# A second MLP's up projection in seven block products instead of eight, in three of its four quarters

## The chip, the core and the metric

The kernel runs on one core of a Trainium2 chip. The metric is the device time of one execution in microseconds (us). The core's engines are named as in the profile: PE (matrix products), with its weight loads shown apart as PEld; DVE, ACT and POOL (elementwise work); SP (it issues DMAs). Each engine takes its instructions strictly in the order of its own program and waits on semaphores.

## The reference, cut to what matters

The reference is a decoder of two layers on 512 positions (SEQ) of width 1024 (D_MODEL); each layer ends in a squared-ReLU MLP of width 4096 (D_FF):

```python
def squared_relu_mlp(h, w_up, w_down):
    return jnp.square(jax.nn.relu(h @ w_up)) @ w_down
...
        x = x + squared_relu_mlp(rmsnorm(x, mlp_norm[layer]), w_up[layer], w_down[layer])
    return x
```

All numbers are float32. The change is in `h @ w_up` of the last layer, a product of 512x1024 by 1024x4096.

## The kernel before, in words

Everything is kept transposed: `self.x` is eight tiles of 128 channels by 512 positions. A float32 product is made from three products of "float32r" halves: each operand is split into a high half (ACT rounds it) and a low half (the rest, a subtraction), and `mm3` issues high x high, high x low and low x high (lines 263, 264, 265). The normalisation's factor per position is applied after the down projection (`r2`, line 1142), so `xg` holds only x times the gain, split in halves.

`mlp(l, ...)` works in four quarters of the hidden width. In a quarter, the up projection makes eight column tiles (`j`): a weight tile of 128x1024 is loaded by SP into a staging buffer (tag `st`, three buffers), `wsplit` makes its halves in a `w` buffer (tag `w`, four buffers; ACT writes the high half, line 256, and DVE or POOL the low half, line 258), 24 matmuls of 128x512 fill one PSUM bank, and ACT and DVE evacuate it (ReLU, square, split into halves; lines 1124, 1125, 300, 301) into `a[j]` (tag `qk`). Then the down projection makes eight tiles (`m`) from the eight `a[j]` in the same way, scales them (1142) and adds them to x (1143). In the second MLP (`l` = 1) the low halves of weights go to DVE and POOL in turn (`"vg"[j % 2]`).

A scheduler of the build places instructions on each engine from this code, and a buffer of a tag goes to the next tile that asks for one when its last reader is done. The only order that counts on the chip is that of each engine's program and of SP's and POOL's DMA issues.

Of the kernel before, what the change touches and what calls it, by code (L numbers as in the profile page):

```python
# [9 lines left out]
F32R = mybir.dt.float32r  # L10
AF = mybir.ActivationFunctionType
ALU = mybir.AluOpType
AX = mybir.AxisListType

P = 128
D = 1024
S = 512
# [16 lines left out]
def bcast(ap, dim, n):  # L34

    a = [list(x) for x in ap.ap]
    a.insert(dim, [0, n])
    return bass.AP(tensor=ap.tensor, offset=ap.offset, ap=a)
# [47 lines left out]
class Work:  # L86
# [5 lines left out]
    def add(self, gen, name=None, when=None):  # L92

        self.q.append(self.mark(self.after(when, gen) if when else gen, name))
# [71 lines left out]
class K:  # L166
    def __init__(self, ctx, tc, ins, out):
# [14 lines left out]
        act=12, st=3, w=4, qk=8, pt4=4, p2=6, raw=2, tmp=3, sq=1, rb=1, tq=2, qki=2, ki=2, x=8, r1=2, r2=2, r3=2, r4=2, r5=2, r6=3, r7=2, nm=8, su=6, cr=6, c1=3, c2=3, nb=4,  # L182
# [3 lines left out]
    def t(self, tag, shape, dt=F32):  # L186
        self.n += 1
        return self.sb.tile(shape, dt, name=f"{self.lab}_{tag}_{self.n}", tag=tag, bufs=self.BUFS[tag])
# [919 lines left out]
    def mlp(self, l, dst, done=None):  # L1108
        nc, ins = self.nc, self.ins
        xg = self.xg(self.x, f"mlp{l}")  # L1110
        side = iter(()) if l else self.presplit()
        r2 = None
        for q in range(4):
            a = []
            for j in range(8):
                w = self.wload(ins["w_up"][l, q * 8 + j], "v" if l == 0 else "vg"[j % 2])
                ps = self.ps(self.pS, [P, S])
                for k in range(KT):
                    self.mm3(
                        ps, [w[:, h, k * P : (k + 1) * P] for h in (0, 1)], [xg[k][:, h, :] for h in (0, 1)],  # L1120
                        k == 0, k == KT - 1,
                    )
                u = self.t("p2", [P, S])
                nc.scalar.activation(u, ps, AF.Relu)  # L1124
                nc.vector.scalar_tensor_tensor(out=u, in0=ps, scalar=0.0, in1=u, op0=ALU.max, op1=ALU.mult)  # L1125
                t = self.t(self.A_TAGS[j], [P, 2, S], F32R)
                self.split(t, u, "v")
                a.append(t)
                if r2 is None:
                    r2 = self.stats_bcast()  # L1130
                elif j % 2:
                    next(side, None)
            for m in range(KT):
                w = self.wload(ins["w_dn"][l, q * 8 + m], "v" if l == 0 else "vg"[m % 2])
                ps = self.ps(self.pS, [P, S])
                for j in range(8):
                    self.mm3(
                        ps, [w[:, h, j * P : (j + 1) * P] for h in (0, 1)], [a[j][:, h, :] for h in (0, 1)],
                        j == 0, j == 7,
                    )  # L1140
                y = self.t("p2", [P, S])
                nc.vector.tensor_tensor(out=y, in0=ps, in1=r2, op=ALU.mult)  # L1142
                nc.vector.tensor_tensor(out=self.x[m], in0=self.x[m], in1=y, op=ALU.add)
                if q < 3 and m < 7:
                    next(side, None)
                if q == 3:
                    nc.sync.dma_start(dst[m], self.x[m])
                    if done:
                        done(m)


    def layer_b(self, xd):
# [415 lines left out]
```

## Time and profile before

| what | us |
|---|---|
| median of three runs | 1364.41 (1364.21 to 1367.28) |
| the profiled execution | 1366.07 |
| its span, first to last instruction | 1364.3 |
| second MLP, from its first matmul to the last (read from the timeline) | about 1008 to 1360 |

The span is what the views below divide; the profiled execution takes 1.8 us more than its span, and is 1.7 us above the median of the runs.

### The profile page before, as it was taken

How to read it: one execution, taken by the hardware profiler on the slowest of the kernel's cores; microseconds unless marked ns; L12 is line 12 of the kernel's file. 1: busy time of each engine (PE TensorE's matmuls, PEld its weight loads, DVE VectorE, ACT ScalarE, POOL GpSimd, SP SyncE). 2: the span in 40 equal slices, each digit the busy share in tenths (PEclk: the TensorE clock that was granted, in tenths of full speed). 3: DMA queues.
4: the chain of work that ended last, by engine and by line, in shares of the span. 5: the costliest groups of instructions: out<-in, count | busy, mean ns of one | idle time of the engine just before them, and what ended most of it. 6: DMA issues, size and time to landing. Idle time of an engine off the chain costs nothing.

```text
span 1364.3 us, 18302 instructions
## 1 busy us (share of the span) xinstructions
PE 1302.6 (95%) x6585; PEld 1071.3 (79%) x6585; DVE 817.3 (60%) x1444; ACT 592.5 (43%) x1364; POOL 461.4 (34%) x574
## 2 busy tenths in 40 slices
PE   7867999999999999999999999999899999999998
PEld 6756887677688888888888788887577888888887
DVE  5976777764588676654555255565578455364452
ACT  6755558674444343321233247666552122222220
POOL 3452684442243333200013576351334222222220
PEclk9987999999999999999999999999999999999999
DMA  6233111012339999923334642224033223223231
GB/s 231 77 101 126 63 40 40 9 34 68 125 115 369 396 316 367 322 98 102 104 117 152 245 151 97 83 90 163 32 123 108 93 93 108 94 94 107 93 107 48
DMA packets 55722, 180.66 MB, mean 132 GB/s; under 512 B 6512, under 2 KB 12656, under 8 KB 54352
## 3 DMA queue, kind: packets, MB, share of 16 engines
q1 hardware_dynamic: 44336, 132.18, 28.4%
q0 software_dynamic: 10720, 46.26, 9.1%
q8 instruction: 52, 0.85, 0.2%
q10 hardware_dynamic: 576, 1.05, 0.2%
q14 instruction: 38, 0.31, 0.1%
HBM read 144.86 MB, written 34.60 MB: 132 GB/s over the span
## 4 chain that ended last, share of the span: by engine, by line
PE 82%; DVE 6%; DMA 5%; ACT 5%; issue 2%; POOL 1%; SPq 0%; ACTq 0%; POOLq 0%; DVEq 0%
PE s_ps L263 19%; PE s_ps L264 19%; PE s_ps L265 19%; PE s_acc L263 4%; PE s_acc L264 4%; PE s_acc L265 4%; PE s_po L1064 2%; DVE s_w L258 1%; DMA s_w<-w_bq 1%; PE s_pt L1051 1%; PE s_ps L1297 1%; PE s_ps L1015 1%; ACT s_w L256 1%; DMA s_st<-in_w_ag_dram 1%; PE s_po L660 1%
## 5 line engine op out<-in xcount | busy, mean ns | idle before, releaser
L256 ACT ACTIVATE s_w<-s_st 128x1024 fp32r<-128x1024 f32 (+2 forms) x182 | 180.4, 996 | 258.2 <-PE s_ps L265 206.3
L263 PE MATMUL s_ps<-s_act,s_w 128*128 128x512 f32 x576 | 223.6, 391 | 1.7 <-ACT s_act L298 1.4
L264 PE MATMUL s_ps<-s_act,s_w 128*128 128x512 f32 x576 | 224.4, 390 | 0.0
L265 PE MATMUL s_ps<-s_act,s_w 128*128 128x512 f32 x576 | 224.1, 390 | 0.0
L258 POOL TENSOR_TENSOR s_w<-s_st,s_w 128x1024 fp32r<-128x1024 f32 (+2 forms) x47 | 105.3, 2242 | 317.7 <-ACT s_w L256 317.7
L264 PE MATMUL s_ps<-s_qk,s_w 128*128 128x512 f32 x512 | 198.5, 389 | 0.0
L265 PE MATMUL s_ps<-s_qk,s_w 128*128 128x512 f32 x512 | 198.5, 389 | 0.0
L263 PE MATMUL s_ps<-s_qk,s_w 128*128 128x512 f32 x512 | 198.1, 389 | 0.0
L258 DVE TENSOR_TENSOR s_w<-s_st,s_w 128x1024 fp32r<-128x1024 f32 (+1 forms) x135 | 164.2, 1221 | 17.7 <-ACT s_w L256 17.1
L1142 DVE TENSOR_TENSOR s_p<-s_ps,s_raw 128x512 f32<-128x512 f32 x64 | 44.2, 691 | 158.3 <-PE s_ps L265 158.3
L1124 ACT ACTIVATE s_p<-s_ps 128x512 f32<-128x512 f32 x64 | 38.2, 598 | 219.8 <-PE s_ps L265 211.8
L263 PEld LDWEIGHTS s_ps<-s_act,s_w 128*128 128x128 f32 x576 | 107.9, 188 | 27.7 <-ACT s_act L298 3.1
L264 PEld LDWEIGHTS s_ps<-s_act,s_w 128*128 128x128 f32 x576 | 108.1, 188 | 23.5 <-issue 0.8
L265 PEld LDWEIGHTS s_ps<-s_act,s_w 128*128 128x128 f32 x576 | 108.1, 188 | 23.2 <-issue 0.8
L263 PE MATMUL s_acc<-s_w,s_act 128*128 128x512 f32 (+3 forms) x304 | 109.6, 363 | 15.7 <-ACT s_w L256 8.3
L1125 DVE SCALAR_TENSOR_TENSOR s_p<-s_ps,s_p 128x512 f32<-128x512 f32 x64 | 44.1, 689 | 122.1 <-ACT s_p L1124 122.1
L263 PEld LDWEIGHTS s_ps<-s_qk,s_w 128*128 128x128 f32 x512 | 96.1, 188 | 20.2
L265 PEld LDWEIGHTS s_ps<-s_qk,s_w 128*128 128x128 f32 x512 | 96.1, 188 | 19.9
L264 PEld LDWEIGHTS s_ps<-s_qk,s_w 128*128 128x128 f32 x512 | 96.1, 188 | 19.9
L264 PE MATMUL s_acc<-s_w,s_act 128*128 128x512 f32 (+3 forms) x304 | 108.4, 357 | 0.7 <-DVE s_w L258 0.6
L265 PE MATMUL s_acc<-s_w,s_act 128*128 128x512 f32 (+3 forms) x304 | 106.4, 354 | 0.0
L696 POOL TENSOR_SCALAR s_p<-s_p,s_cr 128x256 f32<-128x256 f32 (+3 forms) x128 | 69.2, 555 | 79.5 <-DVE s_cr L1027 38.1
(299 smaller groups left out, 2440.2 us busy)
## 6 DMA issues: line engine op xcount, KB each, us to landing
s_st<-in_w_up_dram SPq DMA_DIRECT2D x64, 512.0 KB, 3.5
s_st<-in_w_dn_dram SPq DMA_DIRECT2D x64, 512.0 KB, 3.5
w_bq<-s_pt POOLq DMA_DIRECT2D x32, 384.0 KB, 5.8
s_w<-w_bq SPq DMA_DIRECT2D x16, 768.0 KB, 6.8
w_kv<-s_pt POOLq DMA_DIRECT2D x16, 512.0 KB, 8.5
s_w<-w_kv SPq DMA_DIRECT2D x8, 1024.0 KB, 5.3
s_act<-in_w_bq_dram POOLq DMA_DIRECT2D x16, 384.0 KB, 7.1
w_bo<-s_pt POOLq DMA_DIRECT2D x16, 384.0 KB, 5.8
```

The source lines that it names most:

```text
L256: nc.scalar.activation(w[:, 0], st, AF.Copy)
L258: e.tensor_tensor(out=w[:, 1], in0=st, in1=w[:, 0], op=ALU.subtract)
L263: mm(ps, lh[0], rh[0], start=start, stop=False)
L264: mm(ps, lh[0], rh[1], start=False, stop=False)
L265: mm(ps, lh[1], rh[0], start=False, stop=stop)
L660: nc.tensor.matmul(O[hp * 64 : hp * 64 + 64, :], kf[0][:, kb, 1, hh * HD : (hh + 1) * HD], pT[hh][:, kb, :], start=kb == 0, stop=kb == 1,)
L696: self.nc.gpsimd.tensor_scalar(out=p, in0=p, scalar1=c, scalar2=1.0, op0=ALU.mult, op1=ALU.mult)
L1015: nc.tensor.matmul(Sp, q[:, blk], kk[hl][:, br, 0:n], start=hl == 0, stop=False)
L1064: nc.tensor.matmul(O[x * 64 : x * 64 + 64, q0 + o : q0 + 256], v[:, j, br, :], st[x][br][:, j, o:256], start=half == 0 and br == 0 and j = ...
L1124: nc.scalar.activation(u, ps, AF.Relu)
L1125: nc.vector.scalar_tensor_tensor(out=u, in0=ps, scalar=0.0, in1=u, op0=ALU.max, op1=ALU.mult)
L1142: nc.vector.tensor_tensor(out=y, in0=ps, in1=r2, op=ALU.mult)
```

## The change

In the first quarter nothing changes but that DVE makes all low halves (`"v"`), and that during its down projection `tparts` makes, for four pairs of channel tiles, the four sums of blocks of x*gain that the scheme needs, split in halves; the last of them is written over the second half of `xg[0..3]`. In the other three quarters, `up_pair` makes two column tiles at a time. The product of the pair is seen as 2x2 blocks (channels in two halves, the pair's two columns, positions in two halves of 256), and seven block products of 12 matmuls of 128x256 replace eight: 84 such matmuls in place of 48 of 128x512. For it:

- r is the first column's weights, c a sum of weight blocks that a DMA adds (SP loads the second column into c, then POOL issues a DMA that accumulates two blocks onto it), d a half of the second column, loaded once more into a `qki` buffer;
- `w1`, `w3` and `w4` are the split halves of r, of c, and of r after two additions on DVE (line 1204 of the new file); `w2` those of d;
- the products are added up from PSUM on DVE (line 1204), and ACT makes ReLU and square (1236 to 1243) ahead of the usual split.

PE takes the products in this order: p1 (w1), two with w3 into `p75`, two into `p26` (w1, w4), two into `p43` (w2, w4).

```diff
-                w = self.wload(ins["w_up"][l, q * 8 + j], "v" if l == 0 else "vg"[j % 2])
+            if T:
+                for j in range(0, 8, 2):
+                    a += self.up_pair(l, q * 8 + j, xg, T, self.A_TAGS[j : j + 2])
+            for j in range(0 if not T else 8, 8):
+                w = self.wload(ins["w_up"][l, q * 8 + j], "v")
...
             for m in range(KT):
-                w = self.wload(ins["w_dn"][l, q * 8 + m], "v" if l == 0 else "vg"[m % 2])
+                if l and q == 0 and m < 4:
+                    T.append(self.tparts(xg, m, self.gcol(f"mlp{l}")))
+                w = self.wload(ins["w_dn"][l, q * 8 + m], "v")
...
+    def tparts(self, xg, k, g):
...
+        b1, b2 = [self.t("p2", [P, S]) for _ in range(2)]
+        nc.scalar.activation(b1, self.x[k], AF.Copy, scale=g[:, k : k + 1])
+        nc.scalar.activation(b2, self.x[k + 4], AF.Copy, scale=g[:, k + 4 : k + 5])
...
+    def up_pair(self, l, m, xg, T, tags):
...
+        r = self.wdma(src)
+        c = self.t("st", [P, 2, H * 2])
+        two = lambda a, step: bass.AP(tensor=a.tensor, offset=a.offset, ap=[list(a.ap[0]), [step, 2], [1, 512]])
+        nc.sync.dma_start(c, two(src2, 0))
+        nc.gpsimd.dma_start(c, two(src, src2.offset - src.offset + 512), accum_op=ALU.add)
+        d = self.t("qki", [P, 512])
+        nc.sync.dma_start(d, src2[:, 512:])
+        w1 = self.t("w", [P, 2, 1024], F32R)
+        self.wsplit(w1, r, "v")
+        w2 = self.t("act", [P, 2, 512], F32R)
+        self.wsplit(w2, d, "v")
+        w3 = self.t("w", [P, 2, 1024], F32R)
+        self.wsplit(w3, c.rearrange("p a b -> p (a b)"), "v")
+        add = lambda o, x, y: nc.vector.tensor_tensor(out=o, in0=x, in1=y, op=ALU.add)
+        add(r[:, 0:512], r[:, 0:512], c[:, 1])
+        add(r[:, 512:], r[:, 512:], r[:, 0:512])
+        w4 = self.t("w", [P, 2, 1024], F32R)
+        self.wsplit(w4, r, "v")
...
+        prod(p1, w1, 0, B(0, 0), True, True)
+        nc.scalar.activation(s1, p1, AF.Copy)
+        prod(p75[:, 0], w3, 0, t(2), True, False)
+        prod(p75[:, 1], w3, 512, t(0), False, True)
+        prod(p26[:, 0], w1, 512, B(4, 0), True, False)
+        prod(p26[:, 1], w4, 0, t(1), False, True)
+        u0, u1, v = [self.t("p2", [P, 2, H]) for _ in range(3)]
+        add(u0, p26, bcast(s1, 1, 2))
+        add(v, p75, bcast(u0[:, 1], 1, 2))
+        add(u1[:, 1], p75[:, 1], v[:, 0])
+        prod(p43[:, 0], w2, 0, t(3), True, False)
+        prod(p43[:, 1], w4, 512, B(4, H), False, True)
+        add(v, p43, v)
+        nc.scalar.activation(u0[:, 1], v[:, 1], AF.Relu)
...
+        for u, tag in ((u0, tags[0]), (u1, tags[1])):
+            nc.scalar.activation(u, u, AF.Square)
+            o = self.t(tag, [P, 2, S], F32R)
+            self.split(o, u)
```

What the build makes of it is seen at three places. First SP's queue in the second quarter's up projection; before, it is one load (of 128x1024) a column:

```order
L214 DMA s_st_2338_10728<-in_w_up_dram 128x1024
L214 DMA s_st_2343_10764<-in_w_up_dram 128x1024
L214 DMA s_st_2348_10800<-in_w_up_dram 128x1024
L214 DMA s_st_2353_10836<-in_w_up_dram 128x1024
L214 DMA s_st_2358_10872<-in_w_up_dram 128x1024
```

After it, from the second pair on (`128x2x512` is c, L214 is r, `s_qki` is d; the last rows are the first loads for the down projection). In the built program all four c of a quarter have the same one of the three staging buffers, so the load of the next c waits until DVE has made the low half of this pair's w3:

```order
L1194 DMA s_st_2373_10894<-in_w_up_dram 128x2x512
L214 DMA s_st_2389_11022<-in_w_up_dram 128x1024
L1194 DMA s_st_2390_11024<-in_w_up_dram 128x2x512
L214 DMA s_st_2406_11152<-in_w_up_dram 128x1024
L1197 DMA s_qki_2457_11551<-in_w_up_dram 128x512
L1194 DMA s_st_2407_11154<-in_w_up_dram 128x2x512
L214 DMA s_st_2423_11282<-in_w_dn_dram 128x1024
```

One load per column has become, per pair, three loads here and one accumulating DMA on POOL, and the c are chained. Second, DVE around the fourth pair's weights in the same quarter; `s_st_2406` is its r, `s_st_2407` its c, `s_w_2411` its w3, `s_w_2412` its w4, the two `s_qk` are outputs of the second pair:

```order
L1204 TENSOR_TENSOR s_st_2406_11152<-s_st_2406_11152,s_st_2407_11154 128x512
L1204 TENSOR_TENSOR s_st_2406_11152<-s_st_2406_11152 128x512
L258 TENSOR_TENSOR s_w_2411_11165<-s_st_2407_11154,s_w_2411_11165 128x1024
L301 TENSOR_TENSOR s_qk_2387_11015<-s_p2_2384_10979,s_qk_2387_11015 128x512
L1204 TENSOR_TENSOR s_p2_2401_11109<-s_pt_2398_11045,s_p2_2400_11047 128x512
L301 TENSOR_TENSOR s_qk_2388_11019<-s_p2_2385_10980,s_qk_2388_11019 128x512
L258 TENSOR_TENSOR s_w_2412_11170<-s_st_2406_11152,s_w_2412_11170 128x1024
```

The two additions onto r stand ahead of w3's low half, though w3 does not need them; in the third pair two splits of outputs stand between them and w3 as well. Third, DVE at the end of the second quarter's up projection. Before, it ends with the last column's evacuation, and the down projection's scaling (L1142) follows:

```order
L300 CAST s_qk_2372_10977<-s_p2_2371_10974 128x512
L301 TENSOR_TENSOR s_qk_2372_10977<-s_p2_2371_10974,s_qk_2372_10977 128x512
L1142 TENSOR_TENSOR s_p2_2376_11010<-s_ps_2375_10985,s_raw_2265_10174 128x512
L1143 TENSOR_TENSOR s_x_2117_9618<-s_x_2117_9618,s_p2_2376_11010 128x512
L258 TENSOR_TENSOR s_w_2390_11114<-s_st_2389_11112,s_w_2390_11114 128x1024
```

After it (`s_ps_2416` is the fourth pair's `p43`, the two last `s_qk` are its outputs, `s_w_2436` the fourth weight tile of the down projection, which has the buffer of the fourth pair's w4):

```order
L1204 TENSOR_TENSOR s_p2_2419_11240<-s_ps_2414_11174,s_p2_2420_11241 128x256
L258 TENSOR_TENSOR s_act_2476_11686<-s_qki_2474_11681,s_act_2476_11686 128x512
L258 TENSOR_TENSOR s_w_2436_11383<-s_st_2435_11381,s_w_2436_11383 128x1024
L1204 TENSOR_TENSOR s_p2_2420_11241<-s_ps_2416_11176,s_p2_2420_11241 128x512
L301 TENSOR_TENSOR s_qk_2421_11275<-s_p2_2418_11239,s_qk_2421_11275 128x512
L301 TENSOR_TENSOR s_qk_2422_11279<-s_p2_2419_11240,s_qk_2422_11279 128x512
L1147 TENSOR_TENSOR s_p2_2426_11312<-s_ps_2425_11287,s_raw_2265_10174 128x512
```

The split of a down weight that waits for the last matmul of the fourth pair now stands ahead of that pair's last sum. It stands so in the second and third quarter; in the fourth the sum comes first on DVE, while on ACT the weight's high half stands ahead of the pair's ReLU in all three.

## Rows read from the trace of the kernel before

**Rows 1.** The page: busy time by engine, the chain by engine.
```profile
PE 1302.6 (95%) x6585; PEld 1071.3 (79%) x6585; DVE 817.3 (60%) x1444; ACT 592.5 (43%) x1364; POOL 461.4 (34%) x574
...
PE 82%; DVE 6%; DMA 5%; ACT 5%; issue 2%; POOL 1%; SPq 0%; ACTq 0%; POOLq 0%; DVEq 0%
```

**Rows 2.** Stretches: length, busy us by engine, PE clock, DMA share, GB/s.
```profile
405.00:412.00 7.00, 7.00 (x32) 5.71 (x31) 3.79 (x4) 0.85 (x1) 3.21 (x4) 1.00 0.46 156
412.00:440.00 28.00, 28.00 (x125) 23.07 (x124) 24.04 (x28) 13.46 (x17) 10.06 (x19) 1.00 0.96 368
...
1020.00:1035.00 15.00, 14.73 (x62) 11.21 (x61) 14.90 (x17) 4.88 (x8) 13.12 (x8) 1.00 0.33 105
1035.00:1360.00 325.00, 324.81 (x1433) 268.64 (x1432) 159.89 (x178) 73.00 (x84) 70.69 (x29) 1.00 0.28 93
```

**Rows 3.** Timeline, PE in an up projection: first and last of 22 matmuls.
```profile
1199.85 0.39 PE L263 MATMUL s_ps<-s_act,s_w 128*128 128x512 f32 x1
...
1204.61 0.39 PE L263 MATMUL s_ps<-s_act,s_w 128*128 128x512 f32 x1
```

**Rows 4.** Timeline, PE in layer 1's memory queries: first and last of 22 matmuls.
```profile
925.21 0.28 PE L265 MATMUL s_acc<-s_w,s_act 128*128 128x256 f32 x1
...
927.73 0.28 PE L265 MATMUL s_acc<-s_w,s_act 128*128 128x256 f32 x1
```

**Rows 5.** Groups by shape, 1180 to 1365 us: busy us, mean ns.
```profile
L258 POOL TENSOR_TENSOR s_w<-s_st,s_w 128x1024 fp32r<-128x1024 f32 x15 | 36.7, 2445 | 126.5 <-ACT s_w L256 126.5
L256 ACT ACTIVATE s_w<-s_st 128x1024 fp32r<-128x1024 f32 x30 | 31.7, 1056 | 60.4 <-PE s_ps L265 60.4
...
L258 DVE TENSOR_TENSOR s_w<-s_st,s_w 128x1024 fp32r<-128x1024 f32 x15 | 18.3, 1219 | 0.0
...
L1142 DVE TENSOR_TENSOR s_p<-s_ps,s_raw 128x512 f32<-128x512 f32 x18 | 12.5, 692 | 58.1 <-PE s_ps L265 58.1
...
L1124 ACT ACTIVATE s_p<-s_ps 128x512 f32<-128x512 f32 x16 | 9.6, 599 | 63.2 <-PE s_ps L265 63.2
```

**Rows 6.** Groups by shape, whole span: a 256-wide ACT and DVE operation.
```profile
L525 ACT ACTIVATE s_sq<-s_acc 128x256 f32<-128x256 f32 x12 | 4.7, 389 | 4.3 <-PE s_acc L265 4.3
...
L596 DVE TENSOR_TENSOR s_tq<-s_acc,gr 128x256 f32<-128x256 f32 x8 | 3.4, 420 | 0.1
```

**Rows 7.** Timeline around a column's end: handing on between engines.
```profile
1201.89 0.39 PE L263 MATMUL s_ps<-s_act,s_w 128*128 128x512 f32 x1
...
1202.09 0.60 ACT L1124 ACTIVATE s_p<-s_ps 128x512 f32<-128x512 f32 x1 [3.90 <-PE s_ps L265]
...
1202.58 1.05 ACT L256 ACTIVATE s_w<-s_st 128x1024 fp32r<-128x1024 f32 x1
...
1203.45 0.43 DVE L300 CAST s_qk<-s_p 128x512 fp32r<-128x512 f32 x1
1203.79 1.22 DVE L258 TENSOR_TENSOR s_w<-s_st,s_w 128x1024 fp32r<-128x1024 f32 x1
1204.92 0.69 DVE L301 TENSOR_TENSOR s_qk<-s_p,s_qk 128x512 fp32r<-128x512 f32 x1
...
1205.04 0.33 SPq L214 DMA_DIRECT2D s_st<-in_w_dn_dram  x1
```

**Rows 8.** Weight loads (L214, SP), 1040 to 1364 us: issue to landing.
```profile
DMA to landing us min/median/max: 3.3/3.5/4.4
```

**Rows 9.** POOL's loads (L237): 512 KB at 400 to 412; seven at 410 to 440.
```profile
L237 POOL DMA_DIRECT2D s_act<-in_w_kv_dram x2: 544/563/582, 407.1 to 408.9; - x2
DMA to landing us min/median/max: 4.0/5.0/5.9
...
DMA to landing us min/median/max: 5.8/9.2/10.2
```

**Rows 10.** Timeline, DVE and POOL in the first quarter's up projection.
```profile
1023.94 2.63 DVE L300 CAST s_qk<-s_p 128x512 fp32r<-128x512 f32 x1
...
1023.69 2.59 POOL L258 TENSOR_TENSOR s_w<-s_st,s_w 128x1024 fp32r<-128x1024 f32 x1
```

More of the change, by code (lines that the diff above doesn't have):

```diff
@@ L1111, in mlp @@
         side = iter(()) if l else self.presplit()
-        r2 = None
+        r2, T = None, []
         for q in range(4):
             a = []
-            for j in range(8):
-                w = self.wload(ins["w_up"][l, q * 8 + j], "v" if l == 0 else "vg"[j % 2])
+            if T:
[3 more added lines that the diff above has]
+                w = self.wload(ins["w_up"][l, q * 8 + j], "v")
                 ps = self.ps(self.pS, [P, S])
@@ L1149, in mlp @@
                         done(m)
+    def tparts(self, xg, k, g):
+        nc = self.nc
+        H = S // 2
+        b1, b2 = [self.t("p2", [P, S]) for _ in range(2)]
+        nc.scalar.activation(b1, self.x[k], AF.Copy, scale=g[:, k : k + 1])
+        nc.scalar.activation(b2, self.x[k + 4], AF.Copy, scale=g[:, k + 4 : k + 5])
+        t, u = [self.t("qki", [P, 2, H]) for _ in range(2)]
+        sub = lambda o, x, y: nc.vector.tensor_tensor(out=o, in0=x, in1=y, op=ALU.subtract)
+        sub(t[:, 0], b1[:, 0:H], b1[:, H:])
+        nc.vector.scalar_tensor_tensor(
+            out=t[:, 1], in0=b2[:, H:], scalar=-1.0, in1=t[:, 0], op0=ALU.mult, op1=ALU.subtract
+        )
+        sub(u[:, 0], b2[:, H:], b1[:, H:])
+        nc.vector.scalar_tensor_tensor(
+            out=u[:, 1], in0=t[:, 1], scalar=-1.0, in1=b2[:, 0:H], op0=ALU.mult, op1=ALU.subtract
+        )
+        o = self.t("pt4", [P, 2, 2, H], F32R)
+        self.split(o, t)
+        if k % 2 == 0:
+            self.t3 = self.t("act", [P, 2, 2, H], F32R)
+        o3 = self.t3[:, k % 2]
+        self.split(o3, u[:, 0])
+        o4 = xg[k][:, :, H:]
+        self.split(o4, u[:, 1])
+        return [o[:, :, 0], o[:, :, 1], o3, o4]
@@ new lines, in up_pair, with prod @@
+    def up_pair(self, l, m, xg, T, tags):
+        nc = self.nc
+        H = S // 2
+        src = self.ins["w_up"][l, m]
+        src2 = self.ins["w_up"][l, m + 1]
+        r = self.wdma(src)
[16 more added lines that the diff above has]
+        self.wsplit(w4, r, "v")
+        def prod(ps, w, o, b, start, stop):
+            for p in range(4):
+                bp = b(p)
+                self.mm3(
+                    ps, [w[:, h, o + p * P : o + p * P + P] for h in (0, 1)], [bp(h) for h in (0, 1)],
+                    start and p == 0, stop and p == 3,
+                )
+        B = lambda k0, c0: lambda p: lambda h: xg[p + k0][:, h, c0 : c0 + H]
+        t = lambda i: lambda p: lambda h: T[p][i][:, h]
+        p1 = self.ps(self.pacc, [P, H])
+        p75, p26, p43 = [self.ps(x, [P, 2, H]) for x in (self.pS, self.pT, self.pS)]
+        s1 = self.t("p2", [P, H])
+        prod(p1, w1, 0, B(0, 0), True, True)
[12 more added lines that the diff above has]
+        nc.scalar.activation(u0[:, 1], v[:, 1], AF.Relu)
+        nc.scalar.activation(u0[:, 0], u0[:, 0], AF.Relu)
+        nc.scalar.activation(u1[:, 0], v[:, 0], AF.Relu, scale=-1.0)
+        nc.scalar.activation(u1[:, 1], u1[:, 1], AF.Relu, scale=-1.0)
+        u0, u1 = [x.rearrange("p a b -> p (a b)") for x in (u0, u1)]
+        out = []
+        for u, tag in ((u0, tags[0]), (u1, tags[1])):
+            nc.scalar.activation(u, u, AF.Square)
+            o = self.t(tag, [P, 2, S], F32R)
+            self.split(o, u)
+            out.append(o)
+        return out
```

## The prediction

> **What bounds the kernel now.** I read the page first: PE is busy for 95% of the span and holds 82% of the chain that ended last [rows 1]. That is an average over stages, so I then asked for the stretch of the second MLP: from 1035 to 1360 us PE is busy 324.81 of 325.00, at full clock, while DVE works half the time, ACT a fifth, and the DMA engines 28% [rows 2]. Nothing is waited for there; time is the number of matmuls times their pitch. Two pieces of the timeline give the pitch: 21 steps of a 128x512 matmul take 4.76 us, 0.2267 each [rows 3], and 21 steps of a 128x256 one take 2.52 us, 0.1200 each [rows 4]. Two half-wide matmuls thus cost 0.2400, 6% more than one wide one, and eat half of what seven products in place of eight save.
>
> **The saving on PE.** In three quarters, 3 x 8 x 24 = 576 wide matmuls (130.6 us) become 3 x 4 x 84 = 1008 half-wide ones (121.0 us): 9.6 us less, if PE never waits. A column of the down projection stays 24 x 0.2267 = 5.44 us; a pair of up columns is 10.08 us where it was 10.88.
>
> **The work beside it.** Per pair DVE has three low halves of 1024 (1.22 each), w2's half, two additions onto r, three wide sums from PSUM and two output splits (eight of 0.69), and one 256-wide sum (0.42): 9.6 us in 10.08 [rows 5, 6]. ACT has three of 1.06, five of 0.60 and five of 0.39: about 8.1. Neighbouring DVE operations overlap by 0.09 (1203.79 + 1.22 against 1204.92 [rows 7]), so DVE fits, but hardly. POOL gives up its low halves (2.4 us each) and has one DMA issue per pair (0.54 [rows 9]). What counts is therefore not the sums but the order, and I follow the two places where something comes late.
>
> **First place: the weight sums c.** I set 0 where PE would begin a quarter's first pair. A pair uses w3 1.44 after its start (its low half 0.24 later), frees it at 4.32, and reaches w4 at 5.76. A hand-over to a free DMA queue takes 0.03 (1203.79 + 1.22 to 1205.04), and a plain load lands in 3.5 [rows 7, 8]; I use 0.05 per hand-over. Let A be the accumulating DMA's time to landing.
> - w3 of pair 1 takes a buffer that the sixth down column frees at -10.88; high half to -9.6, low half after that column's scaling to -8.1. So c of pair 2 is loaded by -4.5 and summed by -4.5 + A, well before w3's buffer is free at 4.32. High half to 5.6, low half to 6.8.
> - c of pair 3: issued 6.85, loaded 10.35, summed 10.4 + A. Then two additions that depend on each other (1.4), two output splits (1.2) and w3's low half (1.22): ready at 14.25 + A. PE needs it at 20.16 + 1.68 = 21.84: in time while A is below 7.6.
> - c of pair 4: load and hand-overs 3.65, A, additions 1.4, low half 1.22: ready at 20.5 + 2A. PE needs it at 30.24 + 1.68 = 31.9. A quarter loses 2A - 11.4 us when A is over 5.7, so each microsecond of A beyond that costs 6 us in three quarters.
>
> No accumulating DMA stands in the trace. The nearest rows are POOL's plain loads of 512 KB: 4.0 and 5.9 with the DMA engines at 46%, and 5.8 to 10.2 with them at 96% [rows 2, 9]. In the new up projection a pair moves 1.79 MB in 10.08 us, some 180 GB/s where there are 93 now, so the share should come to about 55%, near the first two. I take the later of these, **A = 5.9**, since the accumulation also reads what it writes; the ends are 4.0 and 10.2. At 5.9 the loss is 0.4 per quarter, 1.2 in all; at 4.0 nothing; at 10.2 27 us.
>
> The Trainium skill speaks against this edit (Collectives: The Full Stack, "The bandwidth ceiling: the fold count and why AG ≠ RS ≠ AR"): a DMA that adds needs two source reads for each piece it delivers, so reading takes twice as long. No row here shows it. By the share in rows 2, an engine moves 93 / (0.28 x 16) = 21 GB/s, 1.6 us for its 32 KB; the rule would add an estimated 1.6 us to a plain load, A = 5.6 to 7.5, and put the kernel between 1359 and 1370.
>
> **Second place: the end of a quarter's up projection.** Let E be when PE would start the down projection. The first down column uses outputs 1 to 6 until E + 4.08, and then the fourth pair's. PSUM is read 0.20 after the last matmul [rows 7]. ACT: the fourth down weight's high half until 1.25. DVE: its low half until 2.64, the pair's last sum until 3.24. ACT again: two ReLUs (4.0), two squares (5.05), high halves of outputs (5.55 and 6.05). DVE: their low halves (6.34, 6.94). PE wants output 7 at 4.08 and finds it at 5.55, its low half 0.56 later still: a loss of 2.0 us. That order holds in the second and third quarter. In the fourth DVE makes the sum first, the low half comes at 4.54 where 4.31 is wanted: 0.2. Together 4.3 us (0 if these chains were hidden; 7 if all three were slow). Before, the last column's evacuation is 2.6 us long (0.60 + 0.69 + 0.43 + 0.69, with waits) against 4.76 until its output is wanted.
>
> **Costs at nothing.** `tparts` puts about 2.9 us on ACT and 3.2 us on DVE into each of four down columns; with the column's own 2.6, DVE has 5.8 in 5.44 us, a lag of 1.5 us at most, which three weight tiles split ahead (16 us) cover; without that cover it would be 1.5. In the first quarter DVE takes over POOL's low halves while it is itself the chain (14.90 of 15.00 busy [rows 2]); but its operations that stand beside POOL's are stretched there, as the cast of 2.63 us [rows 10] that is 0.43 elsewhere [rows 7], so I expect no net change, within 1 us either way (the stretch loses about 1 us of PE now). SP's extra issues are 0.33 each [rows 7] and stand behind nothing that comes later than what they wait for themselves. The clock I leave at its 1.00: the short waits of the first quarter did not lower it [rows 2].
>
> **Sum.** -9.6 + 1.2 + 4.3 = -4.1 us. The profiled execution would go from 1366.1 to 1362.0; it lies 1.7 us above the median of the runs, so on their scale 1364.4 becomes **1360.3**. Changes under 0.3% (4.1 us) can't be told from none here.
>
> **The rivals.**
> 1. *The accumulating DMA is slow.* At A = 8 a quarter loses 4.6 us: -9.6 + 13.8 + 4.3 = +8.5, 1373. For it: it reads its target as well, in rows of 2 KB, and behind two other loads; POOL's loads reach 9 us when traffic is dense. Against it: traffic should be half of that. It decides from A = 6.6 (no gain) and 7.3 (slower by 0.3%).
> 2. *The sums are in time and the ends are hidden better than I count*, for instance because A is 5 and ACT's operations overlap more: -9.6 to -5.3, 1355 to 1359. Against it: the order on DVE and ACT is fixed, and each operation of the chain has a row.
> 3. *Seven products don't save anything on PE.* If the half-wide matmuls ran at 0.1295, the 1008 would take as long as the 576. The trace has 0.1200 with the same three matmuls per operand, but in runs of 24, with activations as the stationary operand. Then +5.5: 1370.
> 4. *DVE becomes the bound.* 9.6 us of work in 10.08, less the overlap, leaves 1.5 us a pair; if its sums from PSUM took 0.2 us more each, the slack would still hold. If it fell, each pair would cost what DVE is over; at +0.5 us on 12 pairs, +6: 1366.
>
> **How the numbers follow.** My case (A from 5.2 to 7.2; 1359 to 1368): 0.42. Rival 1: 0.28; rival 2: 0.20; rivals 3 and 4: 0.05 each. Faster by over 0.3% takes rival 2 and half of my case: 0.41. Slower by over 0.3%: rival 1, rival 3 and a part of my case's upper end: 0.33. Between: 0.26. The range 1355 to 1376 leaves out the very best of rival 2 (0.05) and A beyond 8.5 (0.13).
>
> **What the profile after would show.** The half-wide matmuls 0.120 apart; up projections of 40.3 us plus waits; c's accumulation landing near 6 us after its issue on POOL; PE waiting in the third or fourth pair of a quarter for line 258 on DVE, under 1 us; PE waiting about 2 us for the last outputs at two of three starts of a down projection, little at the third; the first quarter as before within 1 us. Wrong would be a wait in the second pair, an accumulation of 8 us or more, or a pitch above 0.125.

## The result, and the profile after

The changed kernel is slower: 1378.0 us against 1367.6 (medians of eight runs each), a ratio of 1.0066 with a 95% interval of 1.0044 to 1.0088. Forecast were 1360.3 and a range of 1355 to 1376. The profiled executions stand at 1373.76 and 1366.07, spans of 1372.0 and 1364.3, so the trace has 7.7 us to explain.

The page of the changed kernel, beside [rows 1]: PE is busy 3.8 us less, and the chain that ended last runs through PE for 70% of the span, no longer 82%. DMA holds 12% where it had 5, DVE 10% where it had 6.

```profile
PE 1298.8 (95%) x7017; PEld 1088.4 (79%) x7017; DVE 864.4 (63%) x1552; ACT 654.7 (48%) x1492; POOL 394.5 (29%) x554
...
PE 70%; DMA 12%; DVE 10%; ACT 4%; issue 2%; POOL 1%; SPq 0%; POOLq 0%; DVEq 0%; ACTq 0%
```

The stretch of the second MLP after, beside the last of [rows 2] (same columns): PE had 0.2 us idle there, now it has 10.6.

```profile
1035.00:1360.00 325.00, 314.42 (x1838) 279.73 (x1839) 207.86 (x283) 134.76 (x212) 15.86 (x13) 0.99 0.44 124
```

Cut at the first matmul of each up and down projection, the stage is easy to read. Before, each of the three up projections lasts 43.52 us; this is the first of them:

```profile
1098.53:1142.05 43.52, 43.52 (x194) 36.04 (x192) 24.45 (x27) 11.88 (x15) 9.71 (x4) 1.00 0.30 95
```

After, the same three stretches; the first column after the times is the length, the second PE's busy time, and the third from the end PE's granted clock:

```profile
1100.10:1146.80 46.70, 42.84 (x338) 41.88 (x337) 29.61 (x39) 23.68 (x40) 3.64 (x3) 0.96 0.51 132
1190.34:1236.46 46.12, 42.40 (x338) 41.78 (x337) 30.92 (x41) 25.22 (x42) 2.41 (x2) 0.96 0.53 139
1280.00:1323.08 43.08, 40.62 (x338) 40.21 (x337) 28.56 (x37) 23.25 (x40) 2.41 (x2) 1.00 0.50 123
```

They sum to 135.9 where 130.6 stood: 5.3 of the 7.7 us. The rest of the new stage (three down projections and the end) is 0.8 us longer. The other 1.6 us lie ahead of the first pair, where the stage begins 1.6 us later. What PE waited for from 1000 us on (total, times, longest; a wait ahead of the stage is left out):

```profile
PE s_ps L265 <- DVE s_w L258: 5.8, 5, 2.2
PE s_ps L263 <- ACT s_w L256: 4.2, 4, 2.1
...
PE s_ps L264 <- DVE s_qk L301: 0.2, 1, 0.2
```

Ten microseconds of waits are for the two halves of a split weight, all of them for w3, in the third and fourth pair of a quarter (in the last quarter only in the fourth). On the 40.10 us that an up projection takes where nothing is waited for (the runs below) the three lose 15.6: 11.5 in steps from matmul to matmul that hold a wait, the rest in slower steps behind the waits, most of them at half clock. Waits for the outputs of an up projection, of which 4.3 us were forecast, come to 0.2.

One pass round the buffer of c, on the timeline of the second quarter: load issued on SP, accumulating transfer issued on POOL, additions onto r, output splits and w3's low half on DVE, next load.

```profile
1109.74 0.38 SPq L1194 DMA_DIRECT2D s_st<-in_w_up_dram  x1
...
1114.64 1.19 POOL L1195 DMA_DIRECT2D s_st<-in_w_up_dram  x1 [12.79 <-DMA s_st<-in_w_up_dram]
...
1120.83 0.69 DVE L1204 TENSOR_TENSOR s_st<-s_st,s_st 128x512 f32<-128x512 f32 x1 [5.65 <-DMA s_st<-in_w_up_dram]
1121.56 0.69 DVE L1204 TENSOR_TENSOR s_st<-s_st 128x512 f32<-128x512 f32 x1
1122.17 1.28 DVE L301 TENSOR_TENSOR s_qk<-s_p,s_qk 128x512 fp32r<-128x512 f32 x2
1123.37 2.35 DVE L258 TENSOR_TENSOR s_w<-s_st,s_w 128x1024 fp32r<-128x1024 f32 x2
...
1124.62 0.38 SPq L1194 DMA_DIRECT2D s_st<-in_w_up_dram  x1
```

From load to load 14.88 us: 4.90 to the issue on POOL, 6.19 to the first addition, 3.79 to the next load. A pair takes PE 10.0 us. Each pass therefore falls 3.5 to 5 us further behind PE (from the second pair's load on, the passes of this quarter take 14.60, 14.88 and, up to the fourth w3, 13.5), and by the third pair here, by the fourth in the last quarter, the lead from the down projection is used up. The twelve accumulating transfers by their line: time on POOL, and the landing:

```profile
L1195 POOL DMA_DIRECT2D s_st<-in_w_up_dram x12: 1194/1203/1309, 1081.8 to 1305.8; - x12
...
DMA to landing us min/median/max: 6.1/6.4/8.9
```

The plain loads of c ahead of them, by theirs, where [rows 8] have a median of 3.5:

```profile
DMA to landing us min/median/max: 3.6/4.0/5.1
```

The clock shows something I had left out. Two stretches of the new stage stood at half the granted clock (1.2 GHz), each after a wait of over 2 us for w3; behind the shorter waits of this trace it stayed at 1.00. That length alone does not decide: the second trace of this kernel, at the end of the experiments, has two more such stretches behind shorter waits. The first here follows the wait of 2.20 us that ended at 1124.64, the second that of the fourth pair, which the whole row 1226.50 to 1236.46 follows:

```profile
1125.20:1128.60 3.40, 3.40 (x18) 3.40 (x17) 3.37 (x6) 1.95 (x4) 0.00 (x0) 0.51 0.62 210
...
1226.50:1236.46 9.96, 9.96 (x71) 9.96 (x72) 9.22 (x13) 6.96 (x13) 0.00 (x0) 0.83 0.62 200
```

In such a stretch half-wide matmuls come 0.213 us apart (1125.42 to 1128.40 in fourteen steps). The first one cost nothing in the end, since w3 of the next pair was later still. The second cost 1.5 us: these 9.96 us are 8.4 in the last quarter, where the clock stayed up (1314.64 to 1323.08).

### The profile page after: what moved, and what is told of

It is laid out like the page before. It is cut to its first block, busy times and chain, and to the rows that moved or that the text cites. A ratio compares the mean times of both kernels' runs of the same rounds, so it can differ in the third digit from the quotient of the medians.

```text
span 1372.0 us, 19486 instructions
## 1 busy us (share of the span) xinstructions
PE 1298.8 (95%) x7017; PEld 1088.4 (79%) x7017; DVE 864.4 (63%) x1552; ACT 654.7 (48%) x1492; POOL 394.5 (29%) x554
## 4 chain that ended last, share of the span: by engine, by line
PE 70%; DMA 12%; DVE 10%; ACT 4%; issue 2%; POOL 1%; SPq 0%; POOLq 0%; DVEq 0%; ACTq 0%
PE s_ps L263 15%; PE s_ps L265 15%; PE s_ps L264 15%; DMA s_st<-in_w_up_dram 7%; PE s_acc L263 4%; PE s_acc L264 4%; PE s_acc L265 4%; DVE s_w L258 3%; PE s_po L1064 2%; DMA s_w<-w_bq 2%; PE s_pt L1051 1%; PE s_ps L1015 1%; PE s_ps L1395 1%; DVE s_st L1204 1%; ACT s_w L256 1%
## 5 line engine op out<-in xcount | busy, mean ns | idle before, releaser
L256 ACT ACTIVATE s_w<-s_st 128x1024 fp32r<-128x1024 f32 (+2 forms) x194 | 193.1, 1000 | 255.9 <-PE s_ps L265 176.0
L258 DVE TENSOR_TENSOR s_w<-s_st,s_w 128x1024 fp32r<-128x1024 f32 (+1 forms) x179 | 218.7, 1227 | 21.0 <-ACT s_w L256 20.1
L265 PE MATMUL s_ps<-s_act,s_w 128*128 128x512 f32 (+1 forms) x480 | 177.4, 371 | 5.8 <-DVE s_w L258 5.8
L263 PE MATMUL s_ps<-s_act,s_w 128*128 128x512 f32 (+1 forms) x480 | 176.8, 372 | 6.0 <-ACT s_w L256 4.2
L264 PE MATMUL s_ps<-s_act,s_w 128*128 128x512 f32 (+1 forms) x480 | 177.1, 370 | 0.0
L263 PEld LDWEIGHTS s_ps<-s_act,s_w 128*128 128x128 f32 x480 | 90.4, 189 | 25.3 <-ACT s_w L256 5.0
L265 PEld LDWEIGHTS s_ps<-s_act,s_w 128*128 128x128 f32 x480 | 90.9, 189 | 22.6 <-DVE s_w L258 6.9
L264 PEld LDWEIGHTS s_ps<-s_act,s_w 128*128 128x128 f32 x480 | 90.8, 189 | 16.2 <-issue 0.8
L1195 POOL DMA_DIRECT2D s_st<-in_w_up_dram x12 | 14.6, 1214 | 255.7 <-DMA s_st<-in_w_up_dram 84.9
L1127 ACT ACTIVATE s_p<-s_ps 128x512 f32<-128x512 f32 x40 | 23.9, 596 | 127.0 <-PE s_ps L265 124.3
L263 PEld LDWEIGHTS s_acc<-s_w,s_act 128*128 128x128 f32 x304 | 58.9, 194 | 25.8 <-ACT s_w L256 8.1
```

What stands on the lines that cost most here:

```text
L256: nc.scalar.activation(w[:, 0], st, AF.Copy)
L258: e.tensor_tensor(out=w[:, 1], in0=st, in1=w[:, 0], op=ALU.subtract)
L263: mm(ps, lh[0], rh[0], start=start, stop=False)
L264: mm(ps, lh[0], rh[1], start=False, stop=False)
L265: mm(ps, lh[1], rh[0], start=False, stop=stop)
L1195: nc.gpsimd.dma_start(c, two(src, src2.offset - src.offset + 512), accum_op=ALU.add)
```

## The experiments

The theory, from here on A: the sums c return to one buffer; a pass round it (load, accumulating transfer, additions, low half of w3) takes 14 to 16 us against a pair's 10.0, and nothing else makes the kernel slower. Against it: B, DVE or ACT is what is late; Q or T, the traffic or a queue. Where no other is named, the edit is to the changed kernel.

**The transfer left out.**

```
-        nc.gpsimd.dma_start(c, two(src, src2.offset - src.offset + 512), accum_op=ALU.add)
```

> Leaves out the accumulating transfer: the sum tile then holds the second block's left half twice and no part of the first block, so the numbers differ; all other instructions stay. Theory A (the sum tile's own loop is too long: plain load 4.3, issue on GpSimd and accumulating transfer 7.0, two adds 1.4, low half of w3 1.2, together 14 to 15 us against the 10.0 us that a pair takes on TensorE): the loop falls to about 7 us, TensorE no longer waits for w3, each of the three up projections takes 40.1 us in place of 46.7, 46.1 and 43.1, TensorE's granted clock stays at 1.00 there; 15.7 us less than the changed kernel's profiled execution, so 10 us less than the kernel before (about 1357). Theory B (VectorE or ScalarE, which carry 26 us of splits and sums in each 46 us, are what is late): less than 3 us gained on the changed kernel, waits for w3 remain.

1356.9 us, ratio to the kernel before 0.9909 (0.9888 to 0.9930). No wait for w3 is left, and all three up projections take 40.10, the first of them here. B falls: DVE and ACT did the same work.

```profile
1097.08:1137.18 40.10, 40.10 (x338) 40.10 (x336) 33.17 (x43) 26.74 (x45) 0.00 (x0) 1.00 0.38 126
```

**A second buffer for c**, whole computation. c alternates between `st` and `ab`, a tag that this stage leaves unused and that is widened to 4 KB per partition; `nb`, a tag used only ahead of this stage, gets three buffers in place of four.

```
...
-        c = self.t("st", [P, 2, H * 2])
+        c = self.t("st" if m % 4 else "ab", [P, 2, H * 2])
```

> The whole computation; the sum tile alternates between two buffers instead of returning to one, so the next pair's load need not wait for this pair's w3. The accumulating transfers and all bytes stay. Theory A (one buffer closes a loop of 14 to 15 us): the loop now serves two pairs, 7.3 us each, under the 10.0 of a pair: no waits for w3, up projections near 40.1 us, 12 to 16 us less than the changed kernel, so 1357 to 1361 against 1367.6 before. Rival A2 (the accumulating transfers are slow because two reads share the DMA engines or because the queue behind them is held; more of them at once makes each longer): the transfer's 6.4 us grow towards 9 and the gain is under 5 us. Theory B (splits on VectorE and ScalarE): no gain.

1356.05 us, ratio 0.9900 (0.9882 to 0.9919): this version beats both kernels. Its three up projections:

```profile
1097.15:1137.25 40.10, 40.10 (x337) 40.09 (x336) 33.17 (x43) 26.75 (x45) 2.42 (x2) 1.00 0.62 165
1180.80:1220.90 40.10, 40.10 (x338) 40.10 (x336) 33.18 (x43) 26.74 (x45) 2.41 (x2) 1.00 0.61 172
1264.44:1304.54 40.10, 40.10 (x337) 40.09 (x336) 33.98 (x43) 25.64 (x43) 1.20 (x1) 1.00 0.45 129
```

PE is busy all through at full clock. The transfers did not get slower, though the DMA engines are busier in two of the three stretches (0.62 and 0.61 after 0.51 and 0.53): the six into each buffer landed in 6.2 and 6.3 us (medians). So the 6.4 us alone do no harm; returning to one buffer does. Rival A2 falls.

**Only the low halves moved to VectorE**, on the kernel before:

```
-                w = self.wload(ins["w_up"][l, q * 8 + j], "v" if l == 0 else "vg"[j % 2])
+                w = self.wload(ins["w_up"][l, q * 8 + j], "v")
```

> The kernel before with one part of the change alone: in the second MLP every weight's low half is made on VectorE, none on GpSimd (2.4 us there, 1.2 on VectorE). No pair of blocks, no accumulating transfer. Theory A: TensorE is fully busy in that stage and VectorE under 60%, so nothing moves: within 1 us of the kernel before. Rival: the first quarter, whose start lay 1.6 us later in the changed kernel's trace, pays for VectorE doing all low halves beside the normalisation statistics: 1.5 to 2 us slower.

1368.9 against 1369.3, ratio 1.0004 (0.9987 to 1.0020): nothing, as forecast. The late start of the changed kernel's stage is not this edit's.

**The sums on GpSimd, in place**, no accumulating transfer, each block loaded once:

```
+        c = self.wdma(src2)
...
+        self.wsplit(w2, c[:, 512:], "v")
...
+        cadd(c[:, 512:], c[:, 512:], c[:, 0:512])
+        cadd(c[:, 0:512], c[:, 0:512], r[:, 0:512])
```

> The whole computation without any accumulating transfer: the second block is loaded once, as it lies, and the two sums for w3 are added in place on GpSimd (two adds of 128x512 a pair). Half the bytes of the up projection's loads go. Theory A: the chain load 3.5, w2's halves, two GpSimd adds of 1 to 1.3, w3's halves 2.3, two adds 1.4, w4's halves 2.3 is 13 to 15 us long, but its two tiles run round three buffers, so it may last 15 us: no or small waits (under 1 us a pair), up projections 40 to 42 us, 1357 to 1362. Rival A3 (not the transfer but the length of the chain matters, whatever makes the sums): up projections stay at 43 to 46 us, 1366 or more.

1357.7 us, 0.9919 (0.9896 to 0.9942); up projections 40.10, 40.11 and 40.11. Two additions a pair on POOL, each longer than expected:

```profile
L1198 POOL TENSOR_TENSOR s_st<-s_st,s_st 128x512 f32<-128x512 f32 x12 | 18.6, 1552 | 0.9
L1198 POOL TENSOR_TENSOR s_st<-s_st 128x512 f32<-128x512 f32 x12 | 16.2, 1351 | 221.6 <-DVE s_act L258 221.6
```

**The same on VectorE** (`cadd` on `nc.vector`):

> As the version with GpSimd's adds, but the two adds of 128x512 a pair are put on VectorE (0.69 us each, so 5.5 us more in each up projection there, where VectorE was busy 33.4 of 40 us). Theory A (only the loop round the one sum buffer made the change slow): VectorE at 39 of 40 us still just fits; up projections 40.1 to 41, no wait over 0.5 us, 1356 to 1361. Rival B (VectorE is what binds next): TensorE waits for low halves of w3 and w4, up projections 42 us or more, 1363 and above.

1356.7 us, 0.9918 (0.9894 to 0.9942), up projections 40.10 three times, DVE busy 32.7 of each. B falls a second time, and my 39 us of DVE were too many.

**The products of w3 placed later.**

```
-        prod(p75[:, 0], w3, 0, t(2), True, False)
-        prod(p75[:, 1], w3, 512, t(0), False, True)
         prod(p26[:, 0], w1, 512, B(4, 0), True, False)
+        prod(p43[:, 0], w2, 0, t(3), True, False)
+        prod(p75[:, 0], w3, 0, t(2), True, False)
+        prod(p75[:, 1], w3, 512, t(0), False, True)
         prod(p26[:, 1], w4, 0, t(1), False, True)
...
-        prod(p43[:, 0], w2, 0, t(3), True, False)
```

> The whole computation, with the two products that read w3 placed after those that need only w1 and w2: TensorE wants w3 two products, 2.9 us, later in each pair. The loop of 14.6 us is as it was. Theory A: w3 of the fourth pair, which came 6.6, 6.0 and 3.0 us late by its quarter's lost time, comes 3.7, 3.1 and 0.1 late; up projections about 43.5, 43.0 and 40.1, 6 to 9 us gained on the changed kernel, so about 1.5 us above to 2 us below the kernel before. Theory A with the clock: where the waits get shorter TensorE's granted clock may stay at 1.00, which gives another 1.6 us for each stretch at half clock that goes. Rival (what ends the wait is w4 or the buffers, so the order of products is of no use): up projections stay at 46 us.

A miss: 1384.7 us, 1.0108 (1.0081 to 1.0135), where the changed kernel stands at 1.0066 (1.0044 to 1.0088). The waits did not shrink, they moved to a PSUM buffer:

```profile
PE s_ps L263 <- DVE s_p L1204: 9.2, 6, 4.7
PE s_pt L265 <- DVE s_w L258: 4.2, 5, 1.1
PE s_pt L263 <- ACT s_w L256: 2.5, 3, 1.4
```

PE now asks for w3's product and its buffer after others, and the sums that free that buffer stand on DVE behind the addition onto r, for which DVE itself sits waiting for the transfer:

```profile
1129.12 0.69 DVE L1204 TENSOR_TENSOR s_st<-s_st,s_st 128x512 f32<-128x512 f32 x1 [5.20 <-DMA s_st<-in_w_up_dram]
1129.73 0.68 DVE L1204 TENSOR_TENSOR s_p<-s_ps,s_p 128x512 f32<-128x512 f32 x1
```

The up projections took 48.5, 48.0 and 49.4 us at clocks of 0.93 to 0.96. A late loop is not cured by wanting its product later: w4 needs the same sums, and DVE's queue waits with it.

**The transfer as a plain copy** on POOL's queue (nothing is added):

```
-        nc.gpsimd.dma_start(c, two(src, src2.offset - src.offset + 512), accum_op=ALU.add)
+        nc.gpsimd.dma_start(c, two(src, src2.offset - src.offset + 512))
```

> The changed kernel with GpSimd's transfer into the sum tile left as a plain copy that overwrites it (nothing is added, so the sums are wrong); bytes, queue and order as before. By the loop, the fourth pair's w3 is late by 6.6 less three times what a pass gets shorter. Theory Q (the queue behind GpSimd's issue makes the transfer 6.4 us long): 6 us still, up projections 45 to 46.5. Theory S (the adding makes it long, a plain copy takes 4 to 4.5 as on SyncE's queue): a pass of 12.5 us, up projections at 40.1 to 41, 8 us or more gained on the changed kernel.

1356.1 us, 0.9913 (0.9881 to 0.9944), up projections 40.10. The issue occupies POOL 0.72 us in place of 1.20, and the landing falls to:

```profile
L1195 POOL DMA_DIRECT2D s_st<-in_w_up_dram x12: 722/722/779, 1078.4 to 1289.7; - x12
...
DMA to landing us min/median/max: 4.0/4.6/5.4
```

So adding costs 1.8 us of the 6.4, and a pass without it is short enough. Theory S holds; the queue is not what is slow. The Trainium skill's rule that an adding DMA needs two reads for each piece (Collectives: The Full Stack, "The bandwidth ceiling: the fold count and why AG ≠ RS ≠ AR") made an estimated 1.6 us of it in the prediction; the two runs agree with that size. What in the adding takes the time, they do not show.

**Half of the transfer** (256 KB):

```
-        nc.gpsimd.dma_start(c, two(src, src2.offset - src.offset + 512), accum_op=ALU.add)
+        nc.gpsimd.dma_start(c[:, 1], src2[:, 512:], accum_op=ALU.add)
```

> The changed kernel with an accumulating transfer for one half of the sum tile alone, 256 KB in place of 512 KB; the other half stays the second block's left half without the first block's (so that sum is wrong). Theory by bytes: the transfer falls from 6.4 to 3.5 or 4 us, a pass to 12 us, up projections to 40.1, 8 us or more gained on the changed kernel. Theory of a fixed latency: 5.5 to 6 us, a pass of 14 us, up projections 44 to 46, 1 to 5 us gained.

1358.3 us, 0.9928 (0.9904 to 0.9953); up projections 40.89, 40.10 and 40.43:

```profile
DMA to landing us min/median/max: 3.6/4.1/5.2
```

Half the bytes land in 4.1 us in place of 6.4, close to the theory by bytes: 2.3 us for each 256 KB, and some 1.8 besides that bytes do not explain. The gain is the one expected, and the small losses in two quarters say that this pass is just about short enough.

**The same transfers with their terms exchanged**, whole computation, one buffer for c:

```
-        nc.sync.dma_start(c, two(src2, 0))
-        nc.gpsimd.dma_start(c, two(src, src2.offset - src.offset + 512), accum_op=ALU.add)
+        nc.sync.dma_start(c.rearrange("p a b -> p (a b)"), src2)
+        nc.gpsimd.dma_start(c, two(src, src2.offset - src.offset), accum_op=ALU.add)
```

> The whole computation, the changed kernel's one buffer for the sums and its accumulating transfer kept; only which terms come by which transfer is exchanged, so that the plain load into the sum tile brings the second block as it lies (rows of 4 KB, each read once) where it was half of it twice (rows of 2 KB), and the accumulating one brings the two left halves. Theory R (the short rows made the plain load 4.1 us instead of the 3.5 that was forecast): the load lands in 3.5, a pass of the loop is 0.6 us shorter, w3 of the fourth pair 1.8 us less late in each quarter; up projections about 44.8, 44.2 and 41.2, 5 to 7 us gained on the changed kernel. Rival T (the other loads issued beside it make it slow): it stays at 4.0 to 4.2, less than 2 us gained.

1364.0 us, 0.9965 (0.9947 to 0.9984): faster than before, with the loop and its accumulating transfer (6.4 still) in place. The plain load, now rows of 4 KB read once, lands in:

```profile
DMA to landing us min/median/max: 3.1/3.2/4.6
```

The up projections still lose 3.9, 1.2 and 3.0 us on 40.1, half of what they lost (15.6), and at full clock:

```profile
1106.87:1150.88 44.01, 41.06 (x337) 40.29 (x336) 29.61 (x39) 23.67 (x40) 3.58 (x3) 1.00 0.55 139
1194.43:1235.69 41.26, 40.54 (x337) 40.20 (x336) 29.78 (x39) 23.66 (x40) 2.41 (x2) 1.00 0.54 151
1279.24:1322.30 43.06, 40.62 (x338) 40.20 (x337) 28.37 (x37) 23.38 (x40) 2.41 (x2) 1.00 0.49 124
```

Theory R holds: 0.8 us of the plain load was its short, repeated rows. The gain was forecast too small: 5 to 7 us, where the medians of the two kernels differ by 13.9 and these three stretches by 7.6. The traced execution is the slowest of its twelve (1372.96), and its pairs begin only at 1106.87, so what the other runs gained beyond the 7.6 no trace shows. The Trainium skill says that batching 2 KB transfers into 4 KB ones can improve throughput (Perfetto Trace Analysis, "DMA Optimizations"); 4.0 against 3.2 us agrees. Whether the length of the rows or the second read of each counts was not separated.

**The changed kernel again.**

> The changed kernel unaltered, beside the others on one chip, to tell the lost time by the up projections of a second execution. Every theory: 1371 to 1381, slower than before by 0.4 to 0.9%. By the loop theory the waits for w3 come in the third and fourth pair again, 3 to 7 us a quarter; where TensorE's granted clock falls to half behind such a wait is left to vary, and should account for what the runs differ by.

1377.9 us, 1.0058 (1.0036 to 1.0080), with the waits where they were. The traced execution took 1372.85, 0.9 less than the first, but its up projections lost more (8.7, 5.8 and 4.8 us on 40.1); its pairs began 4.1 us earlier:

```profile
1096.02:1144.81 48.79, 44.18 (x338) 43.36 (x336) 30.93 (x41) 24.98 (x42) 3.64 (x3) 0.93 0.50 136
1188.36:1234.22 45.86, 42.58 (x338) 41.82 (x337) 29.61 (x39) 23.79 (x40) 2.41 (x2) 0.96 0.50 134
1277.76:1322.65 44.89, 42.19 (x337) 41.57 (x336) 29.66 (x39) 24.57 (x41) 2.41 (x2) 0.96 0.47 119
```

The clocks of 0.93, 0.96 and 0.96 are two, one and one stretches of 3.4 us at half clock, four where the first trace has two. Two of them followed waits of over 2 us, as there. The other two did not: one came behind waits of 0.55 and 1.00 us for w3, shown here with its row, one behind 1.68 and 1.01; in the first trace 1.45 and 1.00 were followed by none.

```profile
1133.34 0.39 PE L263 MATMUL s_ps<-s_act,s_w 128*128 128x256 f32 x1 [0.55 <-ACT s_w L256]
...
1134.84 0.48 PE L265 MATMUL s_ps<-s_act,s_w 128*128 128x256 f32 x1 [1.00 <-DVE s_w L258]
...
1135.00:1138.40 3.40, 3.40 (x17) 3.40 (x18) 3.40 (x6) 2.43 (x5) 0.00 (x0) 0.50 0.45 152
```

## Why the prediction was wrong

The step that failed is **"First place: the weight sums c"**. The place and the mechanism were right (PE waits for w3 in the third and fourth pair, for lines 256 and 258), but the sum gave it 1.2 us and it cost 15.6, the clock's part included: 46.7, 46.1 and 43.1 us against 40.1. Followed in the second quarter, with 0 at 1100.10, its terms come out so:

- *c of pair 2 was given slack that it did not have.* I had it issued by -8.05 and summed by 1.4, well before a buffer for w3 was free. It was issued at -4.96 and its accumulating transfer only at 0.52, and the additions began at 7.06. The load of c of pair 3 thus left at 9.64, not 6.85: 2.8 us. c of pair 2 was issued late because w3 of pair 1 was: that pair's accumulating transfer landed at -9.44, 8.85 us after its issue, and DVE then scaled an output of the down projection and added it to x ahead of w3's low half. Why POOL issued 1.9 us after the load had landed, no row tells; in both traces of the changed kernel only the first two of the twelve transfers show it.
- *The plain load of c* was put at 3.5 from [rows 8], loads of 4 KB rows with quieter DMA engines. It took 4.90 and 4.60 from its issue to POOL's, where 3.55 and 3.65 were reckoned: 2.3 us in two passes. The load landed 4.33 and 4.04 us after its issue, and POOL issued 0.57 after each landing, where 0.05 was reckoned. With the terms exchanged the same two loads landed in 3.2, so the short, repeated rows explain the landing, and the hand-over is the rest.
- *A* was put at 5.9 and was 6.19 and 6.33 here: 0.7 us. This was the one unknown that I bounded, and the nearest of the three. My condition "over 5.7" for a loss was right in kind, but with the other two terms the limit lies lower: at 4.1 the half transfer still cost 0.8 us in one quarter.

Together 5.8; w3's low half was done at 38.0 where 32.3 was forecast and 31.9 wanted. Rival 1 named the right place and a near time (1373), for an A of 8; the median was 6.4, and only single transfers took as long (8.85 for the second quarter's first pair, 8.41 for the third quarter's second), so its nearness is luck.

**"The clock I leave at its 1.00"** failed as well, and belongs to the same waits: 1.5 us of the 15.6 in the profiled execution. The medians differ by 10.4 us, of which the new stage of the trace explains 6.1 (5.3 + 0.8). In the second trace the stage from the first pair to the end takes 275.1 us, with four stretches at half clock, where the kernel before takes 265.8: 9.3 us more, most of the 10.4. The runs' mean granted clocks fit: 0.976 to 0.979 in six of the first eight runs of the changed kernel and 0.982 in its two fastest, against a median of 0.983 for the kernel before (in its runs beside the experiments) and 0.982 to 0.987 for the version with two buffers. A stretch of 3.4 us at half clock lowers the mean by 0.0012, so 0.005 is an estimated four stretches more. Not all need lie in this stage: from 800 us to the first pair the trace of before has three, those of the changed kernel four and two. What decides whether a short wait is followed by such a stretch stays open.

**"Second place: the end of a quarter's up projection"** was too dear: 4.3 us forecast, 0.2 of waits. I let PE want output 7 after 4.08 us. In the program's order of the second quarter PE runs the first six outputs of two down columns and 11 matmuls of a third ahead of output 7, 47 matmuls or 10.7 us. The fourth pair's low halves came on DVE 8.1 to 9.4 us after the down projection began at 1146.80:

```profile
1154.92 1.29 DVE L301 TENSOR_TENSOR s_qk<-s_p,s_qk 128x512 fp32r<-128x512 f32 x2 [2.35 <-ACT s_qk L298]
```

**What held.** A pair moves 1.84 MB, not 1.79, but the 180 GB/s stand, and the DMA engines' share, forecast at 55%, was 0.50 to 0.53. The saving on PE: 9.6 forecast, 10.3 measured where nothing is waited for (three times 43.52 - 40.10), with half-wide matmuls 0.1193 apart; rival 3 falls. `tparts` cost nothing: the down projection that holds it took 43.52 us before and after. The move of the low halves to DVE cost nothing, by its own run. DVE was not the bound, rival 4, by two runs. The 1.6 us ahead of the pairs are not the change: in its second trace they begin at 1096.02, 2.5 us earlier than the stage does before (1098.53). The kernel with all low halves on VectorE has no pairs and shows such shifts too (its first up projection began at 983.1, the kernel before's at 975.8), while its median is that of the kernel before.

## What to carry to other kernels

Where a buffer is filled, added to, read and filled again, work out the whole pass round it, hand-overs included, and compare it with the time in which its consumer comes back. A pass half again as long as that eats any lead that an idle stretch gave, and either a second buffer or sums in place that rotate through several removes it without a faster step. A load's time is to be taken from a row with the same row length and the same neighbours, and an early term that "has slack" is to be followed as closely as the last. Read the program's order, not the source's, for when an operand is first wanted.

## What the runs showed of the hardware

- An accumulating load of 512 KB from HBM into SBUF takes 6.4 us and 1.20 us of POOL's issue; the same as a plain copy 4.6 and 0.72; 256 KB accumulating 4.1 and 0.87.
- POOL issued a transfer 0.53 to 0.66 us after the landing of the load that it waited for, in ten of twelve cases, and 1.9 after it in the first two.
- At half the granted clock half-wide matmuls come 0.213 us apart, at full clock 0.119. In the two traces of the changed kernel's stage, stretches at half clock followed waits of 0.55 and 1.00, of 1.68 and 1.01, and of 2.1 to 2.2 us; none followed waits of 1.45 and 1.00.
- With half-wide moving operands the weight loads fill the time as well as the matmuls do: PEld is busy 40.10 of 40.10 us in the versions without waits, 36.04 of 43.52 before.
- An addition of 128x512 takes POOL 1.35 to 1.55 us beside DVE, and DVE 0.69.
